# Softmax attention: adding the two halves of P times V ahead of the fold's transposes

## The chip, the cores and the metric

The kernel runs on one core of one Trainium2 chip. The metric is device time in microseconds for one execution, given as the median of several runs. A core has TensorE for matrix products and transposes (PE in the profile, its weight loads PEld), VectorE (DVE), ScalarE (ACT), GpSimd (POOL), and SyncE (SP), which here issues DMAs. Each engine works through its own queue in order and waits on semaphores for the others. Products land in PSUM; the other operands lie in SBUF.

## The reference

The kernel computes a two-layer streaming encoder: 16 learned meta tokens ahead of 1024 frames, so L = 1040 rows of width 1024, in float32. Each layer has a gated linear attention group (GLA) with 4 heads, a softmax attention group (FoX) with 8 heads of 64, an output projection, and a gated feed-forward block with a causal convolution. The change lies in the softmax group:

```python
def block(inp):
    q_b, c_b, start = inp
    logits = (jnp.einsum('bqhd,bkhd->bhqk', q_b, kf)
              + c_b[..., None] - c_k[:, :, None, :])
    q_pos = start + jnp.arange(Q_BLOCK)
    logits = jnp.where(key_pos[None, :] <= q_pos[:, None], logits, -jnp.inf)
    return jnp.einsum('bhqk,bkhd->bqhd', jax.nn.softmax(logits, axis=-1), vf)
...
o_fox = rms_norm(o_fox, fox_norm[i].reshape(FOX_HEADS, FOX_DH)).reshape(B, L, FOX_WIDTH)
h = h + jnp.concatenate([o_gla, o_fox], axis=-1) @ w_out[i]
```

`c` is the running sum of the log forget gates. Each head's output is normalised over its 64 values.

## The kernel before

**Precision.** Matrix products run in a reduced float32 form (fp32r). To keep precision, an operand is split into a high part (a rounded copy, made on ScalarE) and a low part (the rest, a subtraction on VectorE or GpSimd). A dense product of two split operands takes three matmuls (`mm3`, lines 221 to 223). V is split as well, and its halves lie side by side: `V[e]` holds, for each key, 64 columns of the high and 64 of the low part for head e. P, the exponentials, is transposed and split into `PT`.

**The attention loop.** The heads go in four pairs p; e is 0 or 1 within a pair. The 1040 queries are 9 tiles (112 rows for the first, 116 for the others), taken in five groups from the last: (7,8), (5,6), (3,4), (1,2), (0). The loop `fox` walks through 72 steps a layer, one per pair, group, head and tile. A step computes scores into PSUM tiles "S" (lines 658, 659), adds the bias and takes a running minimum on VectorE (L661; signs are turned), and exponentiates on ScalarE with the row sum `den` as a by-product (L673). Later steps do the rest: `fox_transposes` transposes P on TensorE (L694) and splits it (L335 copy, L336 subtraction); `fox_av` multiplies by V (L720); `fox_fold` and `fox_store` finish a group.

**Products with V.** For a head and a group, `fox_av` accumulates into one PSUM tile `av` (pool tag "av", one buffer) with 128 rows: rows 0 to 63 are the products with V's high part, rows 64 to 127 with its low part, one column per query (232 for a group of two tiles, 112 for the first tile). When the last key tile is in, ScalarE copies all 128 rows to `avs[:, e]` in SBUF (L723).

**The fold.** When both heads of a group are done, `fox_fold` transposes `avs` back so that queries are rows: one TensorE transpose for each tile and head (L733) into the PSUM tile `fo` (tag "S", three buffers shared with the scores). Then ScalarE copies the high halves to `f` (L736), VectorE adds the low halves (L737), ScalarE squares (L739), VectorE sums (L743), and a reciprocal root (lines 276 to 280) scales `f` into `on` (L748). `fox_store` transposes `on` once more (L759), and the result goes to DRAM, or for the last pair into the operand of the output projection.

**Order.** Which instruction stands where in each engine's queue is decided in this stage by a scheduler when the program is built; in the feed-forward stages TensorE's order is that of the code. The loop fixes when things are issued: transposes of P two steps after the scores, products three, the fold four, the store six. Between them `work.run` issues filler matmuls: the projections for the next pair of heads (q, k, v), the GLA gate (`gr_products`, lines 613 to 631), and at the end the first tiles of the output projection (`plan(4)`; operands split at L336 as `ml`, result added at L985). One group and head thus takes about 8 us. Weights are split on GpSimd during the attention (L190), and on VectorE once the output projection begins.

Of the kernel before, what the change touches and what calls it, by code (L numbers as in the profile page):

```python
# [10 lines left out]
F32 = mybir.dt.float32  # L11
# [3 lines left out]
ALU = mybir.AluOpType  # L15
# [18 lines left out]
FT, NT, FIRST = 116, 9, 112  # L34
# [100 lines left out]
class Kern:  # L135
# [562 lines left out]
    def fox_av(self, e, tiles, q, PT, avs, pp, part):  # L698
        nc = self.nc
        if part == 0:  # L700
            PT["av"] = pp.tile([128, 256], F32, tag="av", name="av")
        av = PT["av"]
        last = tiles[-1]
        width = FT * (len(tiles) - 1) + self.rows_of(last)
        ts = list(range(4 * part, min(4 * part + 4, last + 1)))
        if part == 0 and last:
            ts[:2] = 1, 0
        for t in ts:
            a, b = 0 if t <= tiles[0] else FT, width
            for i in range(2):  # L710
                if t == NT - 1:
                    w, x = q["Vm"][:, e, :, :], PT[2][:, i, :]
                else:
                    r, p = self.rows_of(t), 3 - t % 4
                    w, x = q["V"][e][:r, t, :, :], PT[part][:r, i, p, a:width]
                    if a == 0 and p < 3:

                        b = 256
                        x = PT[part][:r, i].rearrange("p a b -> p (a b)")[:, 2 * FT * p:2 * FT * p + b]
                nc.tensor.matmul(av[:, a:b], w.rearrange("p a b -> p (a b)"), x,  # L720
                                 start=(t == ts[0] and part == 0 and i == 0), stop=(t == last and i == 1))
        if last < 4 * part + 4:
            nc.scalar.copy(avs[:, e, :width], av[:, :width])  # L723

    def fox_fold(self, tiles, avs, den, ap, pp):
        nc = self.nc
        nt = len(tiles)
        rows = self.rows_of(tiles[0])
        fo = pp.tile([128, 2, 2, 2, 64], F32, tag="S", name="fo")
        for ti in range(nt):  # L730
            for e in range(2):
                w = rows
                nc.tensor.transpose(fo[:w, ti, e].rearrange("p a b -> p (a b)"),  # L733
                                    avs[:, e, FT * ti:FT * ti + w], self.ident[:])
        f = ap.tile([128, 2, 2, 64], F32, tag="ff", name="ff", bufs=1)
        nc.scalar.copy(f[:rows, :nt], fo[:rows, :nt, :, 0])  # L736
        nc.vector.tensor_tensor(out=f[:rows, :nt], in0=fo[:rows, :nt, :, 1], in1=f[:rows, :nt], op=ALU.add)  # L737
        on = sq = ap.tile([128, 2, 2, 64], F32, tag="fon", name="fon", bufs=1)
        nc.scalar.activation(sq[:rows, :nt], f[:rows, :nt], AF.Square)  # L739
        vv, d2, y0, a = (ap.tile([128, 2, 2], F32, tag=f"f{x}", name=f"f{x}", bufs=2)[:rows, :nt] for x in "vdya")  # L740
        nc.vector.scalar_tensor_tensor(out=d2, in0=den[:rows, :nt], scalar=64.0 * EPS,
                                       in1=den[:rows, :nt], op0=ALU.mult, op1=ALU.mult)
        nc.vector.tensor_reduce(out=vv, in_=sq[:rows, :nt], axis=AX.X, op=ALU.add)  # L743
        nc.vector.tensor_tensor(out=vv, in0=vv, in1=d2, op=ALU.add)
        fl = (lambda x: x) if nt == 2 else (lambda x: x[:, 0, :])
        self.rsqrt(fl(y0), fl(vv), fl(y0), fl(a), scale=1.0 / 64)
        for ti in range(nt):
            nc.vector.tensor_tensor(out=on[:rows, ti], in0=f[:rows, ti],  # L748
                                    in1=y0[:, ti, :].unsqueeze(2).to_broadcast([rows, 2, 64]), op=ALU.mult)
        return on  # L750
# [89 lines left out]
    def fox_schedule(self, lyr, at, n, p, e, ti, i, tiles, Ps, st, q, ap, pp, mix3):  # L840
        PT = st[e]

        def T_(ci, P):
            def f():
                if ti == len(tiles) - 1 and ci == 0:
                    for key in range(2):
                        PT[key] = ap.tile([FT, 2, 4, 2 * FT], F32R, tag=f"PT{key}", name=f"PT{key}", bufs=1)
                    if i == NT - 1:
                        PT[2] = ap.tile([FT, 2, FT], F32R, tag="PT2", name="PT2", bufs=1)
                self.fox_transposes(i, ci, P, PT, FT * ti, pp)  # L850
            return f
        for ci, P in enumerate(Ps):
            at(n + 2, f"T{ci}", T_(ci, P))
        if ti == len(tiles) - 1:
            PT["nch"] = len(Ps)
        if ti:
            return

        def av(ci):
            def f():  # L860
                if e == 0 and ci == 0:
                    one = len(tiles) == 1
                    st["avs"] = ap.tile([128, 2, FT if one else 2 * FT], F32, tag="av1" if one else "avs",
                                        name="avs", bufs=1)
                self.fox_av(e, tiles, q, PT, st["avs"], pp, ci)
            return f

        def fold():
            st["on"] = self.fox_fold(tiles, st["avs"], st["den"], ap, pp)

        def store():
            self.fox_store(lyr, p, tiles, st["on"], ap, pp, mix3() if p == 3 else None)
        for ci in range(PT["nch"]):
            at(n + 3, f"av{ci}", av(ci))
        if e == 1:
            at(n + 4, "fold", fold)
            at(n + 6, "store", store)
# [862 lines left out]
```

## Time and profile before

| | |
|---|---|
| median of 3 runs | 2532.57 us (2532.46 to 2533.31) |
| span of the profiled execution | 2534.7 us (its own time is not shown beside the span) |
| attention of layer 0, layer 1 | about 190 to 515 us, 1447 to 1773 us |
| TensorE busy | 2485.4 us (98%), granted clock 0.997 on average |
| VectorE, ScalarE, GpSimd busy | 70%, 50%, 15% |
| DMA | 102 GB/s on average |

A row of instruction groups gives the line in the kernel, the engine and operation, output and input tiles, shape and count, then busy microseconds and the mean nanoseconds of one; behind the bar stands the engine's idle time just before, and who ended it. A row of a timeline gives start and duration in microseconds. A row of waits gives who waited for whom: total microseconds, times, longest. A row of windows gives for each stretch the busy time of the engines with instruction counts, the granted clock as a share of the full one, the DMA share and GB/s. The chain rows give start, duration and the work that the end of the execution is traced back to. TensorE's matmuls overlap in the pipeline, so the duration of one is longer than the distance to the next.

### The profile page before, as it was taken

How to read it: one execution, taken by the hardware profiler on the slowest of the kernel's cores; microseconds unless marked ns; L12 is line 12 of the kernel's file. 1: busy time of each engine (PE TensorE's matmuls, PEld its weight loads, DVE VectorE, ACT ScalarE, POOL GpSimd, SP SyncE). 2: the span in 40 equal slices, each digit the busy share in tenths (PEclk: the TensorE clock that was granted, in tenths of full speed). 3: DMA queues.
4: the chain of work that ended last, by engine and by line, in shares of the span. 5: the costliest groups of instructions: out<-in, count | busy, mean ns of one | idle time of the engine just before them, and what ended most of it. 6: DMA issues, size and time to landing. Idle time of an engine off the chain costs nothing.

```text
span 2534.7 us, 46974 instructions
## 1 busy us (share of the span) xinstructions
PE 2485.4 (98%) x18430; PEld 2383.9 (94%) x18430; DVE 1769.3 (70%) x3508; ACT 1274.8 (50%) x2731; POOL 391.7 (15%) x568
## 2 busy tenths in 40 slices
PE   8999999999999999999999999999999999999998
PEld 7999999999999999999998899999999999997786
DVE  7656776769877777853665666777797777777545
ACT  6346666636444445641343466665464444455312
POOL 3023333210000000100210333331100000001002
PEclk9999999999999999999999999999999999999999
DMA  3232134342322224864312222243423222257622
GB/s 126 64 95 62 51 95 130 119 129 84 118 76 81 82 78 131 201 160 116 102 54 76 74 77 72 67 144 109 147 83 102 76 79 86 76 161 188 182 76 72
DMA packets 117933, 259.75 MB, mean 102 GB/s; under 512 B 14816, under 2 KB 32480, under 8 KB 117712
## 3 DMA queue, kind: packets, MB, share of 16 engines
q1 hardware_dynamic: 93408, 181.74, 23.1%
q0 software_dynamic: 22432, 72.71, 10.4%
q8 instruction: 144, 2.36, 0.4%
q10 hardware_dynamic: 1872, 2.31, 0.3%
q14 instruction: 77, 0.63, 0.1%
HBM read 176.11 MB, written 67.81 MB: 96 GB/s over the span
## 4 chain that ended last, share of the span: by engine, by line
PE 81%; DVE 11%; ACT 4%; DMA 2%; issue 2%; POOL 0%; SPq 0%; DVEq 0%; ACTq 0%; POOLq 0%
PE up L223 10%; PE up L221 10%; PE up L222 10%; PE mm L221 7%; PE mm L223 7%; PE mm L222 7%; PE down L221 5%; PE down L222 5%; PE down L223 5%; PE av L720 3%; PE tr L694 2%; DVE S L661 1%; PE S L658 1%; DVE x L1081 1%; PE S L659 1%
## 5 line engine op out<-in xcount | busy, mean ns | idle before, releaser
L223 PE MATMUL up<-x,hi 128*128 128x260 f32 (+1 forms) x2464 | 697.9, 283 | 4.0 <-DVE x L1081 4.0
L221 PE MATMUL up<-x,hi 128*128 128x260 f32 (+1 forms) x2464 | 698.6, 284 | 2.6 <-ACT x L1080 2.4
L222 PE MATMUL up<-x,lo 128*128 128x260 f32 (+1 forms) x2464 | 697.2, 283 | 0.0
L223 PEld LDWEIGHTS up<-x,hi 128*128 128x128 f32 x2464 | 466.9, 189 | 6.0 <-DVE x L1081 6.0
L221 PEld LDWEIGHTS up<-x,hi 128*128 128x128 f32 x2464 | 465.8, 189 | 3.6 <-ACT x L1080 3.6
L222 PEld LDWEIGHTS up<-x,lo 128*128 128x128 f32 x2464 | 466.2, 189 | 0.1
L1057 DVE TENSOR_TENSOR lo<-raw,hi 128x512 fp32r<-128x512 f32 x364 | 247.9, 686 | 171.6 <-ACT hi L1056 171.6
L221 PE MATMUL mm<-xh,hi 128*128 128x348 f32 (+4 forms) x1056 | 364.3, 345 | 0.0
L223 PE MATMUL mm<-xl,hi 128*128 128x348 f32 (+4 forms) x1056 | 340.2, 322 | 0.0
L222 PE MATMUL mm<-xh,lo 128*128 128x348 f32 (+4 forms) x1056 | 339.5, 322 | 0.0
L1056 ACT CAST hi<-raw 128x512 fp32r<-128x512 f32 x364 | 224.8, 620 | 143.8 <-PE up L223 93.2
L221 PEld LDWEIGHTS mm<-xh,hi 128*128 128x128 f32 x1056 | 200.1, 189 | 5.9 <-issue 5.3
L222 PEld LDWEIGHTS mm<-xh,lo 128*128 128x128 f32 x1056 | 200.1, 189 | 0.4 <-issue 0.3
L223 PEld LDWEIGHTS mm<-xl,hi 128*128 128x128 f32 x1056 | 198.9, 188 | 0.4 <-issue 0.3
L188 ACT CAST hi<-raw 128x512 fp32r<-128x512 f32 (+2 forms) x168 | 97.4, 580 | 182.2 <-PE down L223 105.4
L222 PE MATMUL down<-ah,lo 128*128 128x260 f32 (+1 forms) x528 | 169.0, 320 | 0.1
L221 PE MATMUL down<-ah,hi 128*128 128x260 f32 (+1 forms) x528 | 168.6, 319 | 0.0
L223 PE MATMUL down<-al,hi 128*128 128x260 f32 (+1 forms) x528 | 168.4, 319 | 0.0
L673 ACT ACTIVATE P<-S,m 116x460 f32<-116x460 f32 (+2 forms) x224 | 125.0, 562 | 71.8 <-DVE m L661 68.1
L336 DVE TENSOR_TENSOR PT<-tr,PT 116x464 fp32r<-116x464 f32 (+3 forms) x240 | 123.0, 515 | 47.3 <-ACT PT L335 45.7
L1039 DVE TENSOR_TENSOR raw<-raw,raw 128x512 f32<-128x512 f32 x198 | 129.5, 684 | 18.1 <-DMA raw<-in_wd_dram 15.5
L1270 POOL DMA_DIRECT2D actd<-cv x44 | 23.6, 536 | 764.3 <-DVE cv L1269 743.3
(283 smaller groups left out, 5618.8 us busy)
## 6 DMA issues: line engine op xcount, KB each, us to landing
raw<-in_wm_dram SPq DMA_DIRECT2D x326, 256.0 KB, 2.7
raw<-in_wd_dram SPq DMA_DIRECT2D x64, 256.0 KB, 3.6
actd<-cv POOLq DMA_DIRECT2D x22, 520.0 KB, 3.1
actd<-cv POOLq DMA_DIRECT2D x22, 512.0 KB, 2.9
cb<-cd SPq DMA_DIRECT2D x16, 520.0 KB, 3.7
st<-actd SPq DMA_DIRECT2D x14, 520.0 KB, 4.8
st<-actd SPq DMA_DIRECT2D x14, 512.0 KB, 5.1
kA<-kA SPq DMA_DIRECT2D x24, 260.0 KB, 4.2
```

Of the source, the lines that this page charges most:

```text
L188: nc.scalar.copy(hi[:, :n, :], raw[:, :n, :])
L221: nc.tensor.matmul(ps, wh, xh[:, c0:c0 + n], start=first, stop=False, skip_group_check=more)
L222: nc.tensor.matmul(ps, wl, xh[:, c0:c0 + n], start=False, stop=False, skip_group_check=more)
L223: nc.tensor.matmul(ps, wh, xl[:, c0:c0 + n], start=False, stop=last, skip_group_check=more)
L336: nc.vector.tensor_tensor(out=lo, in0=src, in1=hi.bitcast(F32), op=ALU.subtract)
L658: nc.tensor.matmul(S[:rows, :n], q["qA"][e][:, qs], q["kA"][e][:, c0:k1], start=True, stop=False)
L673: nc.scalar.activation(P[:rows, :n], S[:rows, :n], AF.Exp, scale=-1.0, bias=m[:rows, nch - 1:nch], accum_out=(den if nch == 1 else d3[:row ...
L694: nc.tensor.transpose(tr[:w, 3 - j, :rows], P[:rows, o:o + w], id_)
L720: nc.tensor.matmul(av[:, a:b], w.rearrange("p a b -> p (a b)"), x, start=(t == ts[0] and part == 0 and i == 0), stop=(t == last and i == 1))
L1039: nc.vector.tensor_tensor(out=q[out][:, :nk, :], in0=q[a][:, :nk, :], in1=q[b][:, :nk, :], op=op)
L1056: nc.scalar.copy(hi[:, :nk, :], src[:, :nk, :])
L1057: nc.vector.tensor_tensor(out=lo[:, :nk, :], in0=src[:, :nk, :], in1=hi[:, :nk, :].bitcast(F32), op=ALU.subtract)
```

## The change

`fox_av` now ends with two instructions in place of one: ScalarE copies only the low half of `av` (rows 64 to 127) into `avs`, and VectorE adds the high half (rows 0 to 63, from PSUM) to it in place. `avs` is half as large: head 0 lies in rows 0 to 63, head 1 in rows 64 to 127 of one tile. The fold then needs one transpose for each tile, which brings both heads, and its own add is gone. `fo` is half as large.

```diff
         if last < 4 * part + 4:
-            nc.scalar.copy(avs[:, e, :width], av[:, :width])
+            own = avs[64 * e:64 * e + 64, :width]
+            nc.scalar.copy(own, av[64:128, :width])
+            nc.vector.tensor_tensor(out=own, in0=av[0:64, :width], in1=own, op=ALU.add)
 
     def fox_fold(self, tiles, avs, den, ap, pp):
         nc = self.nc
         nt = len(tiles)
         rows = self.rows_of(tiles[0])
-        fo = pp.tile([128, 2, 2, 2, 64], F32, tag="S", name="fo")
+        fo = pp.tile([128, 2, 2, 64], F32, tag="S", name="fo")
         for ti in range(nt):
-            for e in range(2):
-                w = rows
-                nc.tensor.transpose(fo[:w, ti, e].rearrange("p a b -> p (a b)"),
-                                    avs[:, e, FT * ti:FT * ti + w], self.ident[:])
+            nc.tensor.transpose(fo[:rows, ti].rearrange("p a b -> p (a b)"), avs[:, FT * ti:FT * ti + rows], self.ident[:])
         f = ap.tile([128, 2, 2, 64], F32, tag="ff", name="ff", bufs=1)
-        nc.scalar.copy(f[:rows, :nt], fo[:rows, :nt, :, 0])
-        nc.vector.tensor_tensor(out=f[:rows, :nt], in0=fo[:rows, :nt, :, 1], in1=f[:rows, :nt], op=ALU.add)
+        nc.scalar.copy(f[:rows, :nt], fo[:rows, :nt])
...
-                    st["avs"] = ap.tile([128, 2, FT if one else 2 * FT], F32, tag="av1" if one else "avs",
+                    st["avs"] = ap.tile([128, FT if one else 2 * FT], F32, tag="av1" if one else "avs",
                                         name="avs", bufs=1)
```

## The prediction

> **What bounds the kernel now.** I read the page first (busy time, slices, chain), then PE's waits, then the two attention stretches by window, and last the rows of the fold.
>
> ```profile
> span 2534.7 us, 46974 instructions
> PE 2485.4 (98%) x18430; PEld 2383.9 (94%) x18430; DVE 1769.3 (70%) x3508; ACT 1274.8 (50%) x2731; POOL 391.7 (15%) x568
> PEclk9999999999999999999999999999999999999999
> ```
>
> ```profile
> core 0: us, PE busy (x) PEld busy (x) DVE busy (x) ACT busy (x) POOL busy (x), PEclk, DMA share, GB/s
> 190.00:515.00 325.00, 319.05 (x2250) 307.67 (x2248) 231.84 (x737) 209.90 (x633) 106.55 (x160) 1.00 0.30 90
> 1447.00:1773.00 326.00, 320.12 (x2254) 309.05 (x2255) 232.53 (x738) 210.29 (x634) 105.50 (x158) 1.00 0.29 90
> ```
>
> ```profile
> PE tr L694 <- DVE PT L336: 3.2, 5, 1.2
> PE S L658 <- ACT P L673: 2.2, 4, 0.7
> ```
>
> TensorE is the bound, at the granted clock of 1.00 in both stretches. The softmax attention of layer 0 lies in 190 to 515 us, that of layer 1 in 1447 to 1773 us; in each TensorE is idle for only 6 us. Its waits there are few and short, because the fox loop lays filler matmuls between the attention steps. So an instruction taken from TensorE's queue should shorten the time by the distance to the next start, as long as nothing new makes TensorE wait.
>
> **What is removed.** Each fold of two query tiles sends 4 transposes (L733), each fold of the one first tile 2; after the change 2 and 1. The duration of one (0.272 us) overlaps with the next, so it isn't the price. The chain view and the timeline give the distance.
>
> ```profile
> L733 PE MATMUL fo<-ident,avs 128*116 128x128 f32 x128 | 19.2, 272 | 0.0
> ```
>
> ```profile
> 207.61 0.30 PE tr L694 x3
> 208.98 0.20 PE tr L694 x2
> 209.35 0.44 PE fo L733 x4
> ```
>
> ```profile
> 271.12 0.43 PE L733 MATMUL fo<-ident,avs 128*112 128x128 f32 x2
> 271.31 0.40 PE L223 MATMUL mm<-xl,hi 128*128 128x348 f32 x1
> ```
>
> ```profile
> by line: PE mm L221 14.3%; PE mm L223 13.9%; PE mm L222 13.8%; PE av L720 12.1%; PE tr L694 8.4%; DVE S L661 4.7%; PE S L658 4.2%; PE S L659 4.0%; ACT P L673 3.9%; issue 2.3%; PE fo L733 2.2%; DVE PT L336 1.8%; DMA cb<-cd 1.7%; ACT PT L335
> ```
>
> Four fold transposes hold TensorE 0.44 us, 0.11 each; two of a one-tile fold 0.19 us (271.12 to 271.31), 0.095 each; the similar transposes of P scale with their count (0.20 for two, 0.30 for three). The 128 of the first kind become 64, the 16 of the second 8: 64 x 0.11 + 8 x 0.095 = 7.8 us less TensorE time. From the other side: the chain of layer 0's stretch (last row) has 2.2% of 325 us = 7.2 us in L733, so 14.3 us in both stretches, and half of it is 7.2. I take 7.5 us, 7.2 and 7.8 as its ends.
>
> The Trainium skill, "TensorE: Matmul & The Clock Gate", section "Back-to-back issue gap", gives about 81 ns for each matmul of 128 columns in a stream of weight load and matmul pairs. By it the gain would be 72 x 0.081 = 5.8 us; this trace, with 110 ns for the FP32 transposes, does not agree.
>
> **What is added and moved.** The rows for the other engines:
>
> ```profile
> L723 ACT COPY avs<-av 128x232 f32<-128x232 f32 x64 | 22.8, 356 | 5.1 <-PE av L720 4.2
> L571 ACT CAST qA<-qt 64x348 fp32r<-64x348 f32 x32 | 15.4, 482 | 5.4 <-DVE qt L568 4.7
> L335 ACT CAST PT<-tr 116x348 fp32r<-116x348 f32 x32 | 14.3, 448 | 9.3 <-PE tr L694 9.3
> L336 DVE TENSOR_TENSOR PT<-tr,PT 116x232 fp32r<-116x232 f32 x32 | 12.6, 393 | 5.9 <-ACT PT L335 5.4
> L336 DVE TENSOR_TENSOR PT<-tr,PT 112x112 fp32r<-112x112 f32 x8 | 2.2, 269 | 2.1 <-ACT PT L335 2.1
> L737 DVE TENSOR_TENSOR ff<-fo,ff 116x256 f32<-116x256 f32 x32 | 13.5, 422 | 13.3 <-ACT ff L736 12.1 <-PE S L659 0.4
> L737 DVE TENSOR_TENSOR ff<-fo,ff 112x128 f32<-112x128 f32 x4 | 1.1, 280 | 0.0
> L736 ACT COPY ff<-fo 116x256 f32<-116x256 f32 x32 | 12.0, 374 | 12.4 <-PE fo L733 11.7
> ```
>
> ScalarE: the 80 copies out of av now take 64 rows in place of 128, with as many columns. 64 rows are no cheaper than 116 in L571 against L335 (0.482 and 0.448 us for 348 columns), so I leave them at 0.356; the fold's copy (L736) keeps its 256 columns and 0.374. No cost, no gain. The Square no longer waits for VectorE's add, which shortens the fold's chain; ScalarE is busy 210 of 325 us, so this frees nothing that TensorE waits for, save that fo's PSUM buffer (tag "S") comes free after the copy.
>
> VectorE: 80 adds of PSUM and SBUF, of the size of L336 with 232 and 112 columns: 64 x 0.393 + 16 x 0.269 = 29.5 us. Gone are the 40 adds of the fold (the second L737 row is layer 0's four; 8 in all): 13.5 + 8 x 0.28 = 15.7 us. Net 13.8 us, 6.9 for each stretch: 232 busy us of 325 become 239. That lies beside TensorE's work, with one exception below. No DMA is added or removed; SP's order in the built program is unchanged, POOL's has a few swaps of mask adds and splits. TensorE's order stays too, but for the 72 transposes and some matmuls moved across their neighbours.
>
> The new wait is the add itself: it stands in VectorE's queue behind scans and subtractions and waits for ScalarE's copy, and until it ends the one PSUM buffer "av" is not free for the next head's products, nor may the fold transpose avs. Behind the add queue the scans (L661), on whose minimum the exponentials (L673) wait. Three places decide.
>
> First, the hand-over of av, 80 times. The shortest is at the start of a layer:
>
> ```profile
> 202.42 0.37 ACT L723 COPY avs<-av 128x232 f32<-128x232 f32 x1
> 202.79 0.61 ACT PT L335 x2
> 203.44 0.39 PE L720 MATMUL av<-PT,V 116*128 116x256 f32 x1 [0.35 <-ACT PT L335]
> ```
>
> From the copy's end (202.79) to the next product 0.65 us, more than the add's 0.39; and the built order sets one filler matmul and four transposes more ahead of that product. Cost: 0, with 0.65 as the other end if a scan of 0.64 us is ahead of the add. The next shortest I found:
>
> ```profile
> 259.86 0.23 ACT L723 COPY avs<-av 128x112 f32<-128x112 f32 x1
> 261.57 0.30 PE L720 MATMUL av<-PT,V 112*128 112x112 f32 x1
> ```
>
> 1.5 us, against an add of 0.27: covered.
>
> Second, the first fold of a layer:
>
> ```profile
> 208.68 0.37 ACT L723 COPY avs<-av 128x232 f32<-128x232 f32 x1
> 208.83 0.52 DVE L336 TENSOR_TENSOR PT<-tr,PT 116x348 fp32r<-116x348 f32 x1 [0.18 <-ACT PT L335]
> 209.19 0.60 PE L733 MATMUL fo<-ident,avs 128*116 128x128 f32 x4
> ```
>
> TensorE transposes 0.14 us after the copy ends. In the changed program the add stands behind that subtraction (to 209.35) and takes 0.39: the transposes come at about 209.75, 0.55 us late, less what stands ahead of them in the queue. I take 0.5 per layer, 1.0 in all (ends 0 and 1.2, the latter if the scan goes first).
>
> Third, the end of each attention, where VectorE is the bound for a while:
>
> ```profile
> 455.00:476.00 21.00, 17.58 (x134) 16.69 (x133) 20.88 (x62) 17.97 (x52) 6.20 (x12) 1.00 0.39 114
> 476.00:515.00 39.00, 39.00 (x271) 38.58 (x269) 25.62 (x84) 17.64 (x59) 4.53 (x9) 1.00 0.34 107
> ```
>
> ```profile
> 461.72 0.39 PE L223 MATMUL mm<-ml,hi 128*128 128x256 f32 x1 [1.77 <-DVE ml L336]
> 467.54 0.61 PE L694 MATMUL tr<-ident,P 116*116 116x116 f32 x4 [1.24 <-DVE PT L336]
> ```
>
> From 455 to 476 VectorE is busy 20.9 of 21 us and TensorE idle 3.4. Two or three adds come into it (0.8 to 1.2 us) and one fold's add (0.42) leaves it: 0.4 to 0.8 us more before TensorE goes on. I take 0.4 per layer, 0.8 in all; the ends are 0 and 1.6.
>
> The second head's adds start at partition 64. The Trainium skill, "VectorE: DVE Perf Modes", section "Two Vector instructions with no wait between them", says that an instruction whose operands begin in another quadrant than its predecessors' is held until all earlier ones have finished. No run here shows it yet; with about 0.08 us of overlap lost on either side of two adds per layer in the third place the sum would be some 0.6 us higher.
>
> **The sum.** -7.5 + 0 + 1.0 + 0.8 = -5.7 us. The profiled span is 2534.7 us, 2.1 above the median of 2532.57; it is the only time of that execution that is shown, so I carry the difference over to the median: 2532.6 - 5.7 = 2526.9 us. 0.2% (5.1 us) is about what a measurement of this kernel can tell from no change, and the forecast lies just beyond it, at 0.22%.
>
> **Rivals.** (a) More is won: the adds are all covered, and fo's earlier release and the shorter fold chain take away part of the 2.2 us for which L658 waits. For it: 80 hand-overs with mostly over 1.5 us of cover. Against it: the second place has no cover. -7.8 (the upper end of the gain) - 1.5 at best: 2523.3 to 2525.9 us.
>
> (b) Most is given back: the ends above (0.65 x 2 + 1.2 + 1.6 = 4.1) and up to a further 0.04 us per hand-over in VectorE's queue. For it: VectorE at 71 to 73% of the stretch; against it: TensorE's few waits now. 2528 to 2532.6 us. To the same side leads a transpose that frees less than its distance, 0.08 us each if the 0.19 of two still holds 0.03 of a switch between kinds of matmul: 5.8 in place of 7.5 us, 2528.6.
>
> (c) Slower: one buffer for av, and its release now needs two engines in turn. If each hand-over or fold lost the add's whole length, TensorE would lose 29.5 us: 2532.6 - 7.5 + 29.5 = 2554.6. It decides from (7.5 + 5.1) / 80 = 0.16 us per hand-over. Against it: at 259.86 and in most other places the cover is four times the add.
>
> That the change doesn't do its work I can exclude: the built program has 72 transposes fewer.
>
> **How the numbers follow.** The forecast's own losses are 0.9 to 3.0 us, so 2526 to 2528: chance 0.45, about 0.32 of it under 2527.5. (a) 0.20, (b) 0.25 (0.04 of it the cheaper transposes), (c) 0.10. Faster by over 0.2%: 0.32 + 0.20 = 0.52; within: 0.13 + 0.25 = 0.38; slower: 0.10. The range goes from (a)'s low end to (b)'s high one, 2523.3 to 2532.6, and leaves out (c) and some of the edges.
>
> **What would show it.** After: 72 fold transposes, still near 0.11 us apart; VectorE near 239 us in a stretch of some 322; TensorE's new waits of about half a microsecond at the first fold on the add into avs; the idle time around 455 to 476 up by under 1 us. I am wrong if TensorE waits for that add in many places, if the adds last far over 0.39 us, or if the end of the attention loses microseconds.

## The result, and the profile after

The changed kernel takes 2546.72 us (median of 5 runs, 2542.5 to 2547.5), the kernel before 2533.31 us beside it (2532.46 to 2539.37). The ratio, taken over all five runs of each kernel, is 1.0039, 95% interval 1.0028 to 1.0049: slower by 0.39%, some 10 us, where 0.22% faster was forecast. (The two medians alone would give 0.53%.)

The page of the kernel after, its span and the busy time of each engine:

```profile
span 2540.4 us, 46888 instructions
PE 2480.8 (98%) x18358; PEld 2372.4 (93%) x18358; DVE 1793.2 (71%) x3548; ACT 1282.0 (50%) x2731; POOL 389.3 (15%) x568
```

TensorE has 72 instructions fewer, VectorE 40 more. The instruction groups of the kernel after, with the fold's transposes, the adds and the copies:

```profile
L733 PE MATMUL fo<-ident,avs 128*116 128x128 f32 x64 | 12.4, 275 | 1.3 <-DVE avs L725 1.3
L725 DVE TENSOR_TENSOR avs<-av,avs 64x232 f32<-64x232 f32 x64 | 25.0, 390 | 20.6 <-ACT avs L724 19.6
L724 ACT COPY avs<-av 64x232 f32<-64x232 f32 x64 | 22.3, 348 | 9.7 <-PE av L720 7.7
```

The size of every part came out as forecast: the add takes 0.390 us (0.393 forecast), the copy 0.348 (0.356). Not forecast is what stands behind the second bar of the add: VectorE was idle for 20.6 us ahead of the 64 large adds, 19.6 of them until ScalarE's copy was done. The waits of VectorE and TensorE in the kernel after:

```profile
DVE avs L725 <- ACT avs L724: 22.8, 30, 1.6
```

```profile
PE tr L694 <- DVE PT L336: 6.6, 9, 1.2
PE S L658 <- ACT P L673: 5.5, 10, 0.7
PE av L720 <- DVE PT L336: 2.4, 6, 0.6
PE fo L733 <- DVE avs L725: 1.3, 2, 0.7
```

TensorE's wait for the subtractions of PT has doubled (3.2 before), that for the exponentials more than doubled (2.2 before). The last row, the two first folds, is the only one in which TensorE waits for the add itself.

**The stage as a measure.** The expected effects are a few microseconds in 2535. The parts outside the attention, where the code is the same, differ by up to 8 us between the profiled executions below (1743.6 to 1751.9 us), and the five times of the kernel after alone differ by 5 us, so I measure the attention stage by itself: in each layer from the first score product (L658) to the first product of the up projection. For layer 0, before and after (rows of the timeline: start, duration, engine, line):

```profile
180.10 0.45 PE L658 MATMUL S<-kA,qA 128*116 128x460 f32 x1
572.90 0.29 PE L221 MATMUL up<-x,hi 128*128 128x260 f32 x1
```

```profile
178.72 0.45 PE L658 MATMUL S<-kA,qA 128*116 128x460 f32 x1
577.39 0.29 PE L221 MATMUL up<-x,hi 128*128 128x260 f32 x1
```

392.8 us before, 398.7 after; layer 1 gives 392.6 and 398.2. Both layers together: 785.4 before, 796.8 after, 11.4 more. All runs, measured in this way (the ratio is that of the whole time to the kernel before on the same chip):

| kernel | both stages, us | against before | ratio of times, 95% interval |
|---|---|---|---|
| after | 796.8 | +11.4 | 1.0039 (1.0028 to 1.0049) |
| e1_no_add | 781.1 | -4.3 | 0.9993 (0.9984 to 1.0002) |
| e2_adds_alone | 798.0 | +12.6 | 1.0042 (1.0027 to 1.0057) |
| e3_low_rows | 797.7 | +12.3 | 1.0043 (1.0026 to 1.0059) |
| f1_no_high | 786.4 | +1.0 | 1.0017 (1.0008 to 1.0026) |
| f2_twice | 797.9 | +12.5 | 1.0053 (1.0040 to 1.0065) |
| e5_load | 799.1 | +13.7 | 1.0061 (1.0048 to 1.0074) |
| e6_load_low | 789.2 | +3.8 | 1.0020 (1.0011 to 1.0029) |
| e7_no_chain | 796.5 | +11.1 | 1.0045 (1.0033 to 1.0058) |
| e8_long | 787.5 | +2.1 | 1.0018 (1.0008 to 1.0027) |
| e9_short | 789.2 | +3.8 | 1.0012 (1.0003 to 1.0022) |
| e10_one | 780.5 | -5.0 | 0.9991 (0.9982 to 1.0000) |
| v1_pool | 785.2 | -0.2 | 0.9998 (0.9988 to 1.0007) |
| v6_late_pool | 785.1 | -0.4 | 0.9997 (0.9988 to 1.0006) |
| v1_dve | 783.4 | -2.1 | 0.9994 (0.9985 to 1.0003) |
| v3_late | 783.8 | -1.6 | 0.9994 (0.9985 to 1.0002) |
| v3_late80 | 792.8 | +7.4 | 1.0035 (1.0022 to 1.0048) |
| k5_order | 792.1 | +6.7 | 1.0032 (1.0019 to 1.0044) |
| b_first4 | 789.5 | +4.1 | 1.0010 (1.0001 to 1.0019) |

The stage lengths come from one profile each, taken on several chips. In most kernels the two layers agree within 1 us, in e6_load_low within 2; differences in the table under some 2 us carry no argument. The whole times tell smaller differences less well: by the ratios the kernel after lies 0.46% above e1_no_add, 11.7 us, where the stages differ by 15.7; the other 4 us lie outside the stage, and nothing here explains them.

### The profile page after: what moved, and what is told of

It is laid out like the page before. It is cut to its first block, busy times and chain, and to the rows that moved or that the text cites. A ratio compares the mean times of both kernels' runs of the same rounds, so it can differ in the third digit from the quotient of the medians.

```text
span 2540.4 us, 46888 instructions
## 1 busy us (share of the span) xinstructions
PE 2480.8 (98%) x18358; PEld 2372.4 (93%) x18358; DVE 1793.2 (71%) x3548; ACT 1282.0 (50%) x2731; POOL 389.3 (15%) x568
## 4 chain that ended last, share of the span: by engine, by line
PE 74%; DVE 16%; ACT 6%; issue 2%; DMA 1%; POOL 0%; SPq 0%; DVEq 0%; ACTq 0%; POOLq 0%
PE up L221 10%; PE up L223 10%; PE up L222 10%; PE mm L221 6%; PE mm L223 6%; PE mm L222 6%; PE down L221 5%; PE down L222 5%; PE down L223 5%; DVE S L661 2%; ACT P L673 2%; PE av L720 2%; PE tr L694 1%; DVE PT L336 1%; DVE x L1079 1%
```

## The experiments

**First: which part costs?** e1_no_add is the kernel after without the adds:

```diff
             nc.scalar.copy(own, av[64:128, :width])
-            nc.vector.tensor_tensor(out=own, in0=av[0:64, :width], in1=own, op=ALU.add)
```

> The changed kernel without the 80 adds on VectorE: the high half of P times V is left out, so the result is not the attention's. Theory A (the adds in VectorE's queue cost what is lost: their time, their wait for ScalarE's copy, the held starts): the gain of the 72 transposes shows, 2533 - 7.8 = about 2525.5 us (2523 to 2528). Theory B (the loss comes from the new order of the queues and from TensorE having less work to cover waits with, whoever computes what): 2538 us or more.

e2_adds_alone is the kernel before with the 80 adds, which change what the fold reads:

```diff
             nc.scalar.copy(avs[:, e, :width], av[:, :width])
+            own = avs[64 * e:64 * e + 64, e, :width]
+            nc.vector.tensor_tensor(out=own, in0=av[64 * e:64 * e + 64, :width], in1=own, op=ALU.add)
```

> The kernel before, full copy, four transposes and the fold's own add, plus 80 adds out of av onto a part of avs, of the same size, place and partitions as in the change; they alter the values, so the result is not the attention's. Theory A: the adds cost some 20 us (13 lost plus 7.5 of gain not seen), and 4 more since the fold's add stays: 2550 to 2560 us. Theory B: within 4 us of before, 2530 to 2537 us.

Without the adds the stages take 781.1 us, with the adds alone 798.0. The adds make the loss: 15.7 us of stage time (796.8 - 781.1) in the one pair, 12.6 in the other. And what is left without them is 4.3 us better than before, not 7.8; by the whole times it is not told apart from no gain (0.9993, interval to 1.0002). So e1's median of 2534.2 us misses theory A's 2523 to 2528, and e2's 2547.3 lies just under its 2550.

**Then: is it that the second head's adds are held?** The Trainium skill, "VectorE: DVE Perf Modes", section "Two Vector instructions with no wait between them", says that an instruction whose operands begin in another quadrant than its predecessors' waits until these have finished. The trace agrees: over the 40 adds of each head, the next instruction starts in the median 0.07 us before the end of a first head's add (partition 0) and 0.03 us after the end of a second head's (partition 64). e3_low_rows puts both heads' sums at partition 0, for which the fold needs four transposes of 64 rows again:

```diff
-            own = avs[64 * e:64 * e + 64, :width]
+            own = avs[:, e, :width]
...
-            nc.tensor.transpose(fo[:rows, ti].rearrange("p a b -> p (a b)"), avs[:, FT * ti:FT * ti + rows], self.ident[:])
+            for e in range(2):
+                nc.tensor.transpose(fo[:rows, ti, e], avs[:, e, FT * ti:FT * ti + rows], self.ident[0:64, 0:64])
...
```

> The changed kernel with each head's sum at partitions 0 to 63 of its own columns of avs, and a transpose of 64 rows for each tile and head: the second head's add no longer starts at partition 64. If the held starts of VectorE (0.11 us before and after each of 40 adds, 8.5 us) are a main part of the loss, and a transpose of 64 columns takes half of 0.11 us, about 2541 us; if the hold costs TensorE nothing, as after, 2543 to 2547 us; if a transpose of 64 columns takes TensorE as long as one of 128, up to 7.8 us more than that, 2550 us and over.

797.7 us, as after, though the next instruction now starts 0.07 us before the end of the second head's add too. f2_twice, below, has as many transposes and the held adds, and takes 797.9. So the hold is real, and taking it away where these adds stand gains nothing.

**What are the transposes worth?** f1_no_high is the kernel before without the fold's add (only one half reaches the output); TensorE's work is that of before. f2_twice is the kernel after with each of the fold's transposes issued twice.

```diff
         nc.scalar.copy(f[:rows, :nt], fo[:rows, :nt, :, 0])
-        nc.vector.tensor_tensor(out=f[:rows, :nt], in0=fo[:rows, :nt, :, 1], in1=f[:rows, :nt], op=ALU.add)
```

```diff
-            nc.tensor.transpose(fo[:rows, ti].rearrange("p a b -> p (a b)"), avs[:, FT * ti:FT * ti + rows], self.ident[:])
+            for x in range(2):
+                nc.tensor.transpose(fo[:rows, ti, x].rearrange("p a b -> p (a b)"), avs[:, FT * ti:FT * ti + rows], self.ident[:])
...
```

> The kernel before without the add of L737: the high and low halves are transposed as before, but only one half reaches the output (the other is left out). TensorE's work is that of before, VectorE has 15.7 us less. Against e1_no_add it differs by the 72 fold transposes and by the tiles alone. Theory T (an instruction taken from TensorE's queue shortens the time by what it takes there, 7.8 us): 2540 to 2544, that is e1_no_add plus 7.8, which would put it above the kernel before and so asks for a loss somewhere else; or the kernel before within 1 us if VectorE's 15.7 us are free. Theory V (both engines lead in turn, and VectorE's time counts about 0.4 of itself, as the adds' did: 12 us for 30): 2528 to 2531, below the kernel before by 4 to 7 us and below e1_no_add.

> The kernel after with each of its fold's transposes issued twice, the second into another part of the same tile and not read: TensorE has the transposes of before again, every other engine has the work of after. Theory T (TensorE's time counts in full): 7 to 8 us above the kernel after, 2553 to 2556. Theory V (TensorE waits elsewhere for that long anyway, and its time counts a third or less): 0 to 3 us above it, 2546 to 2550.

Where no adds lie in the way, 72 transposes are worth 786.4 - 781.1 = 5.3 us of the 7.8 (f1 against e1, which differ in the rows of the copy too; 6.1 us by the ratios). Beside the adds they are worth 1.1, which one profile can't tell from nothing (f2 against after; 3.5 us by the ratios, whose intervals overlap): TensorE then waits elsewhere for most of that time. And the 15.7 us of VectorE that the fold's add took are worth nothing: f1 is not below before.

**Load, or place?** e5_load and e6_load_low replace each add by one on scratch tiles in SBUF, at the add's partitions or all at partition 0; e7_no_chain reads av but not the copy's result. The first cut is e5_load's (e6 has `self.scr[0:64, :, :width]`), the second e7_no_chain's; the scratch tile is made and zeroed once a layer, which is left out here.

```diff
-            nc.vector.tensor_tensor(out=own, in0=av[0:64, :width], in1=own, op=ALU.add)
+            x = self.scr[64 * e:64 * e + 64, :, :width]
+            nc.vector.tensor_tensor(out=x[:, 0], in0=x[:, 1], in1=x[:, 0], op=ALU.add)
```

```diff
-            nc.vector.tensor_tensor(out=own, in0=av[0:64, :width], in1=own, op=ALU.add)
+            x = self.scr[64 * e:64 * e + 64, :, :width]
+            nc.vector.tensor_tensor(out=x[:, 0], in0=av[0:64, :width], in1=x[:, 1], op=ALU.add)
```

> The kernel after, in which each of the 80 adds is put onto a scratch tile of SBUF: same place in VectorE's queue, same 64 partitions (0 to 63 for head 0, 64 to 127 for head 1) and the same width, but it waits for no copy and no copy's reader waits for it. The high half of P times V is left out of the output. e1_no_add, the same without the 80 operations, took 2534.2 us, the kernel after 2546.7. Theory L (load: the 30 us of VectorE time itself makes PT's subtractions late): 2543 to 2547. Theory Q (the adds stand at the head of VectorE's queue until ScalarE's copy is there, 22.8 us in all, and PT's subtractions stand behind them): 2533 to 2537. Theory H (what costs is that the adds of head 1 neither start early nor let the next start early, 8.5 us in all): 2538 to 2543, and e6_load_low 4 us or more below this run.

> e5_load with all 80 scratch operations at partitions 0 to 63. Theory L: within 2 us of e5_load, both 2543 to 2547. Theory Q: 2533 to 2537, as e5_load. Theory H: 4 us or more below e5_load, since the adds of head 1 then overlap with their neighbours by 0.07 us on either side instead of standing 0.03 us apart.

> The kernel after, in which each add still reads the low half from PSUM at the same place, but takes its other operand from a zeroed scratch tile of SBUF and writes to a scratch tile: it waits for TensorE's product, as the copy does, and not for the copy, and nothing waits for its result but the next use of the buffer av. The low half of P times V is left out of the output. Unlike the scratch operations of e5_load it can't be moved ahead of its group's product. Theory Q (the chain product, copy, add at the head of VectorE's queue costs, 22.8 us of waits): 2535 to 2539, the kernel without adds (2534.2) plus little. Theory L (VectorE's 30 us by themselves cost, wherever their operands come from): 2544 to 2548. By the stage alone (attention of both layers, 785.4 us before, 796.9 after, 781.1 without adds): Q 782 to 787, L 794 to 798.

(In e7_no_chain and in e8, e9 and e10 below it is the high half that is left out where there is no add; their texts say the low one.) None of the three tested the adds' load in the adds' own places. The rows of e5_load by tile and of e7_no_chain's VectorE by waits:

```profile
L726 DVE TENSOR_TENSOR scr<-scr x80: 258/394/1446, 187.0 to 1489.4; 64x232 f32<-64x232 f32 x64, 64x112 f32<-64x112 f32 x16
```

```profile
DVE scr L726 <- ACT avs L724: 22.8, 30, 1.6
```

The scratch adds wait for nothing, and the scheduler put all 40 of a layer at its beginning: the last starts at 1489.4 us, 47.5 us into layer 1's stage, which lasts 400. e5's whole loss arises in those 47 us: it lies 8.9 us behind the kernel before at 50 us and 6.7 at the end of layer 0. Crowded adds cost, but how much VectorE time in the adds' own places costs, these two don't tell. What they do tell is that the hold can cost: e6, with all its adds crowded in the first 46 us of the stage as well but at partition 0, takes 9.9 us less than e5 (789.2 and 799.1; 0.41% by the ratios), as theory H expected of the pair; the order on VectorE differs a little between the two as well. And e7's add still waits for the copy, with the same 22.8 us and 30 times: the built program evidently keeps two engines that read one PSUM tile in order. In its waits it is the kernel after once more, and so nearly a repetition: 796.5 against 796.8.

**Where in the stage?** e8_long keeps the adds in the groups (7,8), (5,6), (3,4), e9_short in (1,2) and (0), e10_one in (1,2) for the second head alone.

```diff
-            nc.vector.tensor_tensor(out=own, in0=av[0:64, :width], in1=own, op=ALU.add)
+            if last >= 4:
+                nc.vector.tensor_tensor(out=own, in0=av[0:64, :width], in1=own, op=ALU.add)
```

(e9: `last < 4`; e10: `last == 2 and e`.)

> The kernel after with the add in the groups of tiles (7,8), (5,6) and (3,4) alone: 48 adds of 80, 18.8 us of VectorE; in the groups (1,2) and (0) the low half is left out of the output. Between the kernel without adds and the kernel after lie 12.5 us (15.8 in the attention stages). Theory P (the loss sits where one head pair gives way to the next, since short groups follow each other there and each one's add stands ahead of PT's subtractions): 2535 to 2539, stage 783 to 788. Theory N (each add costs the same, 0.16 to 0.20 us): 2541 to 2543, stage 789 to 792.

> The kernel after with the add in the groups (1,2) and (0) alone: 32 adds of 80, 10.4 us of VectorE; in the other groups the low half is left out of the output. Theory P: most of the loss is still there, 2542 to 2546, stage 790 to 795, with the delay against the kernel before growing in steps at the three changes of head pair. Theory N: 2538 to 2540, stage 786 to 788.

> The kernel without adds, with the add put back for group (1,2) and its second head alone: 8 adds, 3.1 us of VectorE; elsewhere the low half is left out of the output. It is the add that, at three of four places in a layer, stands in VectorE's queue ahead of the first row maximum of the next head pair. TensorE's instructions and their order are those of the kernel without adds (stage 781.1). Theory P: a step of 0.7 to 1.5 us at each of the 6 changes of pair, stage 785 to 790. Theory N (0.2 us an add): 782 to 783.5.

How far a score product (L658) of layer 0 starts behind the same product of the kernel before, counted from the start of the stage and worked out from the timelines (us; a choice of every 6th product; columns: the time into the stage before, the last one its end; the pair of heads changes at 74, 155 and 237):

```
into the stage   50    74    82   114   132   155   164   195   214   237   246   300   393
after           0.6   0.4   1.7   1.6   2.2   1.9   3.2   3.0   4.0   3.8   5.7   5.2   5.9
e1_no_add      -0.2  -0.4  -0.4  -0.6  -0.9  -1.2  -1.2  -1.5  -1.7  -2.0  -2.0  -2.5  -2.5
e8_long         0.6   0.5   0.5   0.2   0.7   0.5   0.5   0.2   0.7   0.4   0.5   0.5   1.1
e9_short       -0.2  -0.4   0.9   1.0   0.8   0.6   1.9   1.5   1.4   1.1   3.0   2.1   2.1
v3_late80       0.4   0.2   0.4   0.1   1.1   0.9   1.1   0.8   1.8   1.6   1.8   2.7   3.6
k5_order        0.6   0.4   0.8   0.7   1.3   1.0   1.5   1.3   2.0   1.7   2.8   2.8   3.4
b_first4       -0.0   0.0   1.2   0.5   0.5   0.5   1.7   1.0   1.1   1.1   2.3   1.7   1.8
```

The loss is not spread over the adds; it comes in steps, and e8 and e9 share them out. The 48 adds of the long groups make those between 114 and 132 and between 195 and 214 us, the 32 short ones those at the three changes of head pair; the two losses, 6.4 and 8.1 us above e1, sum up to 14.5 of the 15.7. (The whole times of the two, 2540.9 and 2537.4 us, stand the other way round, since the parts outside the attention differ by more: 1748.6 and 1744.9 us in the profiles.) e10's 8 adds make no step, although they stand right ahead of the next pair's first row minimum: that guess of mine fell. So the steps have two kinds. The traces show a cause for the first, and for a part of the second.

**The step in the middle of a pair: an add in a chain without slack.** The timeline of VectorE in e1_no_add, and in e8_long the same place, the second head of (7,8) (start, duration):

```profile
286.09 0.52 DVE L336 TENSOR_TENSOR PT<-tr,PT 116x348 fp32r<-116x348 f32 x1 [0.18 <-ACT PT L335]
286.58 0.52 DVE L568 SCALAR_TENSOR_TENSOR qt<-mm,r 128x348 f32<-128x348 f32 x1
287.01 0.63 DVE L661 CUSTOM_DVE_ANT_0 S<-S,cb 116x460 f32<-116x460 f32 x1
```

```profile
287.15 0.52 DVE L336 TENSOR_TENSOR PT<-tr,PT 116x348 fp32r<-116x348 f32 x1 [0.19 <-ACT PT L335]
287.70 0.39 DVE L726 TENSOR_TENSOR avs<-av,avs 64x232 f32<-64x232 f32 x1
288.12 0.52 DVE L568 SCALAR_TENSOR_TENSOR qt<-mm,r 128x348 f32<-128x348 f32 x1
288.56 0.64 DVE L661 CUSTOM_DVE_ANT_0 S<-S,cb 116x460 f32<-116x460 f32 x1
```

The add waits for nothing here, but the row minimum behind it comes 0.48 us later: 0.39 for the add and 0.09 for the hold (0.03 us of pause on either side of it, and the 0.03 by which L568 overlaps its predecessor in e1). VectorE lags e1 by 1.06 us ahead of the add and by 1.54 behind it. TensorE lags by 0.76, and goes on with filler products until, 12 us later, it needs a buffer of `tr` that a subtraction of PT gives back, further down the chain of row minimum, exponential, transpose, copy and subtraction. TensorE in e1_no_add and in e8_long:

```profile
295.69 0.37 PE L658 MATMUL S<-kA,qA 128*116 128x460 f32 x1
298.66 0.19 PEld L694 LDWEIGHTS tr<-ident,P 116*116 116x116 f32 x2 [0.26 <-DVE PT L336]
298.66 0.41 PE L694 MATMUL tr<-ident,P 116*116 116x116 f32 x2
```

```profile
296.45 0.37 PE L658 MATMUL S<-kA,qA 128*116 128x460 f32 x1
300.19 0.41 PE L694 MATMUL tr<-ident,P 116*116 116x116 f32 x2 [0.82 <-DVE PT L336]
```

In e1 the chain arrives just in time (the weight load waits 0.26 us); the two adds of the group make it 0.8 us late, and TensorE pays all of it. In the kernel after the same transposes wait 0.92 us, and 1.16 in the next pair.

**The step at the change of pair: the scheduler's order.** VectorE's timeline of the kernel after at the first change of pair, second tile of the new pair (L661 of its first and of its second part, and what lies between):

```profile
258.44 0.63 DVE L661 CUSTOM_DVE_ANT_0 S<-S,cb 116x460 f32<-116x460 f32 x1
...
259.42 0.26 DVE L725 TENSOR_TENSOR avs<-av,avs 64x112 f32<-64x112 f32 x1
259.67 0.52 DVE L626 SCALAR_TENSOR_TENSOR ge<-ge,gy 128x344 f32<-128x344 f32 x1
260.10 0.28 DVE L336 TENSOR_TENSOR V<-tr,V 116x128 fp32r<-116x128 f32 x1
260.30 0.51 DVE L627 SCALAR_TENSOR_TENSOR gy<-ge,gy 128x344 f32<-128x344 f32 x1
260.73 0.22 DVE L336 TENSOR_TENSOR Vm<-tr,Vm 116x64 fp32r<-116x64 f32 x1
260.86 0.50 DVE L629 SCALAR_TENSOR_TENSOR gog<-gy,gog 128x344 f32<-128x344 f32 x1
261.29 0.70 DVE L661 CUSTOM_DVE_ANT_0 S<-S,cb,m 116x464 f32<-116x464 f32 x1
```

and of the kernel before:

```profile
259.35 0.64 DVE L661 CUSTOM_DVE_ANT_0 S<-S,cb 116x460 f32<-116x460 f32 x1
...
260.22 0.71 DVE L661 CUSTOM_DVE_ANT_0 S<-S,cb,m 116x464 f32<-116x464 f32 x1
```

Before, the second part follows the first by 0.87 us, after by 2.85: not for the add (0.26) alone, but for five instructions of the gate and of the V split, 1.6 us from the first one's start to L661's, which stand ahead of it in the scheduler's new order. The same distance is 2.6 to 2.9 us in after, e2, e3, e7, e9 and f2, the kernels with an add right behind the copy for both heads of the short groups, and 0.9 to 1.3 in all others up to then, v3_late80 with its later adds among them. k5_order takes the order back and keeps the adds; b_first4 brings it into the kernel before, without an add:

```diff
-                with self.tc.high_priority(8):
+                with self.tc.high_priority(12 if g == 0 and e == 0 and p and ti == 0 else 8):
```

(b_first4: 4 in place of 12, in the kernel before.)

> The kernel after with its scheduler's priority for the scores raised from 8 to 12 in one step of each head pair but the first (first group, first head, second tile): the same instructions on every engine, all 80 adds among them. In VectorE's queue the row minimum (L661) of that step's second part stands two places behind the first part again, as before, in place of eight. Theory O (the scheduler's new order on VectorE makes the steps at the changes of pair): the 6 steps go, 1.3 to 1.9 us each; stage 786 to 790 against after's 796.9, time 2537 to 2541. Theory L (VectorE's 30 us of adds cost, wherever the others stand): stage 795 to 798, time 2545 to 2548.

> The kernel before with that priority lowered from 8 to 4 in the same steps: no add, the same instructions as before on every engine, but in VectorE's queue the same eight instructions stand between the two parts of the row minimum as in the kernel after (and two more behind the next). Theory O: a step of 1.3 to 1.9 us at each of the 6 changes of pair, stage 793 to 798 against before's 785.4, time 2542 to 2547. Theory L: no step, stage 784 to 787, time as the kernel before within 2 us.

k5 gains 4.7 us of stage, from 796.8 to 792.1, and b_first4 loses 4.1 without any add. (By the ratios k5 and after are not told apart: 1.0032 and 1.0039, with overlapping intervals.) Each is about half of what theory O expected: in k5 a step of 0.4 to 1.1 us stays at each change of pair, in b_first4 up to 0.8 of each step of 1.2 is won back in the 20 us behind it. b_first4's new waits of TensorE:

```profile
PE S L658 <- DVE ff L737: 3.7, 6, 0.7
```

One at each of the six changes, 0.6 us each, for the tile "S" that the fold's add gives back. The kernel after has no such add, so b_first4 shows what the order can cost, and not the wait by which it costs in the kernel after. Order is thus worth 4 to 5 us, and the adds must answer for the rest of the loss at this place. Some of it shows in k5, at five of the six changes:

```profile
PE av L720 <- DVE avs L725: 1.4, 5, 0.3
```

With the scores early again, TensorE comes to the next product with V before the add has freed the buffer av. In layer 0 the product starts 0.27 to 0.29 us late by this wait, and its distance to the instruction before it is 0.5 us longer than in e1.

**Versions with fewer or other adds.** ScalarE copies both halves to SBUF, and one add for both heads follows, on VectorE right behind the copies (v1_dve) or called a step later (v3_late), on GpSimd (v1_pool, v6_late_pool), or called late as two adds of 64 rows (v3_late80). The cut shows v1_dve against the kernel after:

```diff
-            own = avs[64 * e:64 * e + 64, :width]
-            nc.scalar.copy(own, av[64:128, :width])
-            nc.vector.tensor_tensor(out=own, in0=av[0:64, :width], in1=own, op=ALU.add)
+            own = slice(64 * e, 64 * e + 64)
+            nc.scalar.copy(avs[own, 0, :width], av[64:128, :width])
+            nc.scalar.copy(avs[own, 1, :width], av[0:64, :width])
+            if e:
+                nc.vector.tensor_tensor(out=avs[:, 0, :width], in0=avs[:, 1, :width], in1=avs[:, 0, :width], op=ALU.add)
...
```

> Merged transposes, but ScalarE copies both halves of av (64 rows each) to the two parts of avs, and GpSimd adds them once per group: VectorE is rid of the 80 adds and of the fold's 40. Theory A: 2523 to 2530 us, the higher end if ScalarE's 80 copies more (28 us) delay the exponentials. Theory B: 2538 us or more.

> The kernel after with ScalarE copying both halves of each head to SBUF (two copies of 64 partitions) and one VectorE add of 128 partitions for both heads, issued at the start of the next step but one of the planner ahead of the fold, by when both copies have long ended: TensorE has after's work, VectorE 40 adds in place of 80 and no add that waits, ScalarE 80 copies more (28 us). Theory Q: the wait for the copy is what costs, so 2531 to 2537, stage 780 to 786. Theory L: half of the load, half of the loss: 2539 to 2541, stage 788 to 790. Either way the second copy holds the buffer av 0.35 us longer, which cost 2 us per layer at the next product where GpSimd made the add.

> v3_late with the 40 adds of 128 partitions issued where the kernel after issues them, right behind the second head's copies, in place of one planner's step later: the same instructions on every engine, the adds' place alone differs. Theory P (place: an add that comes at the head of VectorE's queue just ahead of a row maximum or a PT subtraction that TensorE will wait for costs its wait and its time): most of after's loss for the second heads comes back, stage 787 to 793 against v3_late's 783.8, with steps at the three changes of head pair; time 2537 to 2542. Theory L (40 adds cost half of what 80 cost, wherever they stand): as v3_late, 782 to 786.

> v3_late with each add of 128 partitions cut in two of 64, one for each head: 80 adds, some 30 us of VectorE as in the kernel after, at the late place. Theory P: within 2 us of v3_late, stage 782 to 787, time 2532 to 2537. Theory L: the other half of the loss appears, stage 790 to 796, time 2540 to 2546.

> v3_late with the 40 late adds on GpSimd in place of VectorE. Theory P: VectorE's late adds cost nothing already, so as v3_late within 2 us, stage 782 to 786, time 2532 to 2536. Theory L: VectorE's 15.7 us go, so below v3_late by 2 to 4 us, stage 779 to 782, time 2529 to 2532.

v1_dve and v3_late are alike (783.4 and 783.8, so v1_dve's theory P failed): the place of the call hardly matters, since in the groups (7,8), (5,6) and (3,4) the scheduler sets nearly all of them at the same places in VectorE's queue. v3_late80 with its 80 adds loses 9.0 us against v3_late's 40, as theory L expected. v1_pool, at 2535.3 us, lies between the ranges of its two theories. VectorE's and TensorE's waits of v1_dve, and those of v3_late80:

```profile
DVE avs L727 <- ACT avs L725: 9.9, 14, 1.0
PE tr L694 <- DVE PT L336: 3.9, 8, 0.9
```

```profile
DVE avs L872 <- ACT avs L725: 27.8, 32, 2.0
PE tr L694 <- DVE PT L336: 8.1, 8, 1.4
```

Forty adds of 128 rows wait less than half as often, and TensorE's wait for PT stays near the 3.2 us of before; with eighty it doubles. v3_late80 has hardly a step at the changes of pair, where its order is before's (1.0 us between the parts): its loss is of the first kind. v1_dve and v3_late, at a ratio of 0.9994, are not told apart from the kernel before. None of them shows the whole of what the TensorE time would give: v6_late_pool, with no add on VectorE at all, is 3.9 us above e1 in the stage. Its TensorE waits 2.0 us for GpSimd's add at the two first folds, and its products with V wait 4.4 us for PT, 0.5 in e1. Whether the second copy, which holds the buffer av longer, is behind the latter was not shown.

## Why the prediction was wrong

**TensorE's gain.** As a distance it was right: TensorE's time in the fold, start to start, goes from 6.7 to 2.8 us per layer, 7.8 in both. As a gain it was over-sized. "An instruction taken from TensorE's queue should shorten the time by the distance to the next start, as long as nothing new makes TensorE wait" holds for 5.3 of 7.8 us alone, and for 1.1 beside the adds (by the stages). The few waits of TensorE before were read as slack of the other engines; in e1's row the chain of VectorE and ScalarE arrives on the spot.

**"That lies beside TensorE's work, with one exception": the step that failed.** VectorE's net 13.8 us were well counted and wrongly covered. The adds cost 15.7 us of stage time (11.7 by the whole times) in place of the 1.8 forecast. Three readings went wrong. The share of busy time (232 of 325 us) was taken as room, where the row minimum, the exponential, P's transposes and PT's split hang on each other, and an add ahead of L661 goes through to TensorE whole (0.48 us). "Behind the add queue the scans" was written down and not priced. And of the built order the prediction named what changed on TensorE, GpSimd and SyncE, and nothing on VectorE, where the scheduler's order changed, for 4 to 5 us.

**The hand-over of av, cost 0**: right for the kernel after. Its products (L720) have no wait for the add in the waits of TensorE. In k5_order they have, 1.4 us in five places: with the order of before kept, this term would not have been 0. The price of 0.16 us per hand-over from which rival (c) decides was passed, with 15.7/80 = 0.2, but not by its mechanism.

**The first fold, 0.5 us per layer**: right in place and near in size, 0.66 and 0.64 us, the row of two waits with 1.3.

**The end of the attention, 0.4 us per layer**: too small. Between 455 and 492 us TensorE is idle for 3.4 us before and 4.3 after, by the windows of layer 0, 0.9 more, just above this term's upper end of 0.8. The loss is not there.

**The hold, 0.6 us**: the rule holds in every second head's add, not only in two per layer. It is 0.09 of the 0.48 us; e3 shows no gain from its removal.

**Rivals.** (b), most given back, and (c), slower, were weighted 0.25 and 0.10; the sign is (c)'s. In (b), "up to a further 0.04 us per hand-over in VectorE's queue" is the term that came nearest to the cause, five times too small.

**The signs of being wrong.** Of the three, none came clearly: TensorE waits for the add in two places alone, the adds last 0.390 us, and the end of the attention loses 0.9 us in layer 0. The delay reaches TensorE under other names, as waits for the subtraction of PT and for the exponential behind the adds.

**The loss accounted for.** Twice layer 0's steps against e1: 9.0 us at the changes of pair (4.7 of them the order, by k5), 4.2 at the two places in mid-pair, 1.6 in the first 50 us and 1.4 behind the last change: 16.2 us, against the 15.7 of both layers. The listed waits add up to less. The stage of layer 0 without the adds, and in the kernel after:

```profile
178.39:568.71 390.32, 383.10 (x2733) 369.18 (x2731) 272.70 (x802) 244.48 (x697) 118.93 (x181) 1.00 0.33 99
178.72:577.39 398.67, 385.58 (x2733) 369.34 (x2731) 288.21 (x842) 243.60 (x697) 118.32 (x181) 1.00 0.32 98
```

TensorE has the same instructions at the same granted clock, yet its busy time (the first figure behind the length) grows by 2.5 us and its idle time by 5.9. After a wait the overlap with the matmul before it is lost, and as the end of that matmul is modelled, a part of the pause counts as busy: at the last change of pair a score product waits 0.67 us by its row and starts 0.92 us later behind its predecessor than in e1. What stays open is most of the 4.3 us at the changes of pair that are not the order, of which k5's five waits for the buffer av are the part that was seen, and what VectorE's time alone would cost in the adds' own places, since e5, e6 and e7 didn't test it.

## What to carry to other kernels

Where a scheduler fills a busy engine with other work, few waits there don't mean that the engines feeding it have slack: before counting an instruction as hidden, follow the chain through its own engine's queue to the next thing that the bound engine will need, and add its time there. Compare the built order on every engine, not only on the bound one; here an added instruction of 0.26 us came with five others moved ahead of a row minimum, 1.6 us. And an experiment that adds load has to be tied to its place by its operands, or the scheduler will put it elsewhere.

## What the runs showed of the hardware

A transpose of 64 rows in FP32 takes TensorE no less time than one of 128: in e3_low_rows the fold takes 7.4 us per layer for 72 transposes, 0.3 of it a wait, and 6.7 before. A copy or an add of 64 partitions is hardly cheaper than one of 128: 0.348 us against 0.356 on ScalarE, 0.390 against 0.397 on VectorE (v1_dve, both operands in SBUF), so that the same sums cost half the time when both heads are added at once.
